# Hymba-style encoder block: one SBUF ring moved by 64 bytes, and four buffers of the up-projection swapped between two rings

## The chip, the cores and the metric

The kernel runs on one core of one Trainium2 chip. The metric is device time in microseconds (us) for one launch, that is for the whole block on one sequence of 2048 tokens. Less is better.

## The reference

```python
def mixer_layer(x, ...):          # convolution group and bidirectional gated linear attention (GLA)
    z = rms_norm(x, mix_norm) @ w_in
    ...
    return concat([y_conv, y_gla]) @ w_out

def memory_cross_attention(x, mem, ...):      # 4 heads of 256, 256 memory rows
    hq = rms_norm(x, xa_norm) @ w_xq
    km, vm = split(rms_norm(mem, mem_norm) @ w_xkv)
    p = softmax(einsum('bqhd,bmhd->bhqm', qh, kh) / 16)
    return einsum('bhqm,bmhd->bqhd', p, vh) @ w_xo

def sq_relu_mlp(x, ...):                      # 1024 -> 4096 -> 1024
    return square(relu(rms_norm(x, mlp_norm) @ w_up)) @ w_down

x = x + mixer_layer(x); x = x + memory_cross_attention(x); x = x + sq_relu_mlp(x)
out = rms_norm(x, final_norm)                 # x: (1, 2048, 1024), all float32
```

## The kernel before, in words

**Products.** Activations lie transposed, with features on the partitions. A product is kept near float32 accuracy by splitting each operand into a rounded part `hi` and a rest `lo` (`split`, line 112: ScalarE copies `hi`, VectorE subtracts to get `lo`) and adding three matmuls, hi·hi, hi·lo and lo·hi (`mm3`, lines 141 to 143; `product`, line 1009; the down-projection, line 1240). In `nc.tensor.matmul(ps, L, R)` the second argument is the stationary operand, 128 columns of weights that are loaded first, and the third is the moving operand, 256 or 512 columns. The profile writes a matmul as `out<-moving,stationary`, and drops digits from tile names: `a` is a tile of the ring A4, `g` of G4, `gt` of GT, `t` of T2, `st` of ST; `ps` and `pg` are PSUM tiles.

**Rings.** All working tiles come from one SBUF pool, `big`. Tiles with one tag share a ring of `bufs` equal buffers. Within a ring, buffers go to tiles in the order in which the program first writes them. The rings lie one after another in the order in which the program first uses them: T2 (7 buffers of 2048 bytes per partition), G4 (8 of 4096), GT (8 of 2048), RAW (3 of 4096), A4 (28 of 4096), SM (11 of 64), ST (2 of 8192), CV (3 of 4112) and GS (9 of 64). In the compiled program T2, G4, GT, RAW and A4 all start 64 bytes past a multiple of 128. SM is 704 bytes long, which is 64 past a multiple of 128, so ST starts on a multiple of 128. Every matmul operand lies at a multiple of 512 bytes from the start of its tile; its address mod 128 is therefore that of its ring.

**Stages, in order of the profile's time.** Up to 850 us: the keys' and values' weights folded with the memory (`kv_mm`; the moving operand `memT` is in GT, 256 wide), the input projection in two halves (in `vg`, the moving weights are 256 wide and lie in A4 and ST by turns), GLA and convolution. From 850 to 1060 us: `w_out` for four blocks of 512 tokens (`y_tiles` puts the moving operand of block 2 half into ST and half into GT). From 1060 to 1431 us: cross-attention in 8 steps of 256 tokens. `xa_scores` multiplies by the folded keys (512 wide, six of eight weight tiles in A4 and two in ST as the moving operand; the stationary operand is in A4, G4 or, for step 1, in GT). `xa_probs` transposes the probabilities and splits them into eight GT tiles `L["p"]`. `xa_out` and, for the last step, `xa_last` multiply them (moving, 256 wide, GT) by the folded values `wO` (stationary, A4 for six of eight tiles, G4 for two).

**Up-projection**, 1431 to 2081 us: for each half `hf` of the tokens and each `f` of 16 pairs of weight tiles, seven Strassen-like products of 12 matmuls, numbered 1, 4, 5, 6, 2, 7, 3 in the order of the code. `weight_side(f + 1)` is written at the head of iteration f: it loads two weight tiles into RAW and CV, forms the sums t1, t2, t4, t3 on VectorE and splits everything: `ha`, `hc`, `hb` into G4, and the operand of product 3, `hd`, into two tiles of ring T, which is GT by default. `c1`, `u2`, `c11` and `c22` (all T2) collect the four outputs, which pass through the squared relu and go to HBM. The last `weight_side(0)` of the first half is written after the outputs of f = 15. `weight_side(0, T2)`, called once before the loop, has its sums and `hd` in T2.

**Down-projection**, 2081 to 2630 us: weights are loaded into T2 (`raw`, line 1164; half of the loads into GT) and split into G4; then the remainder and the final norm.

**Order of the work.** Except in blocks marked as a manual schedule, a planner reorders instructions when the kernel is built: it takes each engine's instructions as they become ready by its own costs, the earlier-written first, and an instruction that is the first to write a tile waits for that tile's turn in its ring. The order is then fixed, and each engine runs its list in that order. The up-projection and the cross-attention are ordered by the planner on all engines.

Of the kernel before, what the change touches and what calls it, by code (L numbers as in the profile page):

```python
# [9 lines left out]
F32 = mybir.dt.float32  # L10
F32R = mybir.dt.float32r
# [6 lines left out]
P = 128  # L18
# [12 lines left out]
def block_kernel(ctx, tc, x, mem, wm, wv, wlg, wlog, wout, wxk, wxv, wxqT, wxo, wup, wdn,  # L31
# [3 lines left out]
    big = ctx.enter_context(tc.tile_pool(name="big", bufs=1))  # L35
# [8 lines left out]
    def G4(dt=F32, shape=(P, 1024)):  # L44
        return big.tile(list(shape), dt, tag="g", name="g4", bufs=NG)
# [10 lines left out]
    def T2(dt=F32, shape=(P, 512)):  # L56
        return big.tile(list(shape), dt, tag="t2", name="t2", bufs=7)

    def GT(dt=F32, shape=(P, 512)):
        return big.tile(list(shape), dt, tag="gt", name="gt", bufs=8)  # L60
# [7 lines left out]
    def PS(shape=(P, 512)):  # L68
        return psp.tile(list(shape), F32, tag="ps", name="ps", bufs=4)

    def PG(shape=(P, 512)):
        return psp.tile(list(shape), F32, tag="pg", name="pg", bufs=4)
# [39 lines left out]
    def split(src, hi, lo):  # L112
        mark["act"] = nc.scalar.copy(hi, src)  # L113
        nc.vector.tensor_tensor(out=lo, in0=src, in1=hi.bitcast(F32), op=ALU.subtract)  # L114
# [403 lines left out]
    def mem_part(q):  # L518
        mt = G4(F32, (P, 4, NMEM))
        nc.sync.dma_start(mt, mem[q * TB:(q + 1) * TB, :].rearrange("(k p) t -> p k t", p=P))  # L520
        for j in range(2):
            hi, lo = GT(F32R, (P, 2, NMEM)), GT(F32R, (P, 2, NMEM))
            for i in range(2):
                kt = 4 * q + 2 * j + i
                if q == 0:
                    nc.scalar.activation(hi[:, i], mt[:, 2 * j + i], AF.Copy, scale=g_mem[:, kt:kt + 1])
                else:
                    nc.vector.tensor_scalar_mul(hi[:, i], mt[:, 2 * j + i], g_mem[:, kt:kt + 1])
                nc.vector.scalar_tensor_tensor(out=lo[:, i], in0=mt[:, 2 * j + i], scalar=g_mem[:, kt:kt + 1],
                                               in1=hi[:, i].bitcast(F32), op0=ALU.mult, op1=ALU.subtract)  # L530
            memT.append((hi, lo))
        return mt
# [126 lines left out]
    def x2_rows(b, i):  # L659
        nc.scalar.copy(rows[:, i], to_rows(rcol[:, 4 * b:4 * b + 4], PS))  # L660
# [99 lines left out]

    with tc.manual_schedule(engines={EngineType.PE}):
        mts = [mem_part(0)]
        ws = [load_w(wxk[0])]
        mts.append(mem_part(1))
        ws.append(load_w(wxk[1]))
        nc.sync.dma_start(cst, consts)
# [156 lines left out]
    def add(out, a, b, op=ALU.add, eng=nc.vector):  # L923
        eng.tensor_tensor(out=out, in0=a, in1=b, op=op)  # L924
# [15 lines left out]
    def R2():  # L940
        return [RAW(), CV()[:, :D]]
# [18 lines left out]
    def token_side(hf):  # L960

        a11 = quarter(hf, 0, 0, S2())
        a22 = quarter(hf, 1, 1, R2())
        a21 = quarter(hf, 1, 0, S2())
        yield None
        yield 1, operand(a11)
        yield 4, operand(a22)
        s = a22  # L970
        both(s, a21, a22, ALU.add)
        yield 5, operand(s)
        both(s, s, a11, ALU.subtract)
        yield 6, operand(s)
        both(a21, a11, a21, ALU.subtract)
        a12 = quarter(hf, 0, 1, S2())
        yield 2, operand(a12)
        yield 7, operand(a21)
        both(a12, a12, s, ALU.subtract)
        yield 3, operand(a12)  # L980

    def weight_side(f, T=GT):

        raw = R2()
        for i in range(2):
            nc.sync.dma_start(raw[i], wup[f + 16 * i])
        w11, w21, w12, w22 = raw[0][:, :TB], raw[0][:, TB:], raw[1][:, :TB], raw[1][:, TB:]
        ha, hc, hb = ([G4(F32R), G4(F32R)] for _ in range(3))
        t1, t2, t4, t3 = T(), T(), T(), T()
        hd = T(F32R), T(F32R)  # L990
        half = lambda h, i: (h[0][:, i * TB:(i + 1) * TB], h[1][:, i * TB:(i + 1) * TB])
        split(raw[0], *ha)
        add(t1, w12, w11, ALU.subtract)
        add(t2, w22, t1, ALU.subtract)
        add(t4, t2, w21, ALU.subtract)
        add(t3, w22, w12, ALU.subtract)
        split(t4, *half(hc, 0))
        split(t3, *half(hc, 1))
        split(t1, *half(hb, 0))
        split(t2, *half(hb, 1))  # L1000
        split(w22, *hd)
        return {1: half(ha, 0), 2: half(ha, 1), 5: half(hb, 0), 6: half(hb, 1), 4: half(hc, 0), 7: half(hc, 1), 3: hd}

    def product(ps, W, X, first):

        for kt in range(4):
            ks = slice(kt * P, (kt + 1) * P)
            for w, x in ((0, 0), (0, 1), (1, 0)):
                nc.tensor.matmul(ps, W[w][:, ks], X[x][kt], start=first and kt + w + x == 0,  # L1009
                                 stop=kt == 3 and w == 1, skip_group_check=not first)  # L1010

    def sq_relu(t, src, f, b):
        nc.scalar.activation(t, src, AF.Relu)
        nc.scalar.activation(t, t, AF.Square)
        nc.sync.dma_start(zu[f * P:(f + 1) * P, b * TB:(b + 1) * TB], t)

    def sq_relu_v(t, f, b):
        nc.vector.scalar_tensor_tensor(out=t, in0=t, scalar=0.0, in1=t, op0=ALU.max, op1=ALU.mult)
        nc.sync.dma_start(zu[f * P:(f + 1) * P, b * TB:(b + 1) * TB], t)
# [8 lines left out]
    for s in range(NS):  # L1028
        if s + 1 < NS:
            xa_scores(s + 1, 0, 0)  # L1030
            if s > 0:
                xa_probs(s, 0)
            xa_scores(s + 1, 0, 1)
            if s > 0:
                xa_probs(s, 1)
                x2_rstd(s - 1)
            xa_scores(s + 1, 1, 0)
            xa_scores(s + 1, 1, 1)
            if s == 0:
                xa_probs(s, 0)  # L1040
                xa_probs(s, 1)
        else:
            xa_probs(s, 0)
            xa_probs(s, 1)
            x2_rstd(s - 1)
            sides = [token_side(0)]
            next(sides[0])
            X = dict([next(sides[0])])
            W = weight_side(0, T2)
            X.update([next(sides[0])])  # L1050
            xa_last(s)
            f_last = sumsq(live[s]["xs"])
            continue
# [12 lines left out]
    for hf in range(2):  # L1066
        b0, b1 = 2 * hf, 2 * hf + 1
        if hf == 1:
            X = {}
        for f in range(16):  # L1070
            def x(i):
                if i not in X:
                    k, X[k] = next(sides[hf])
                    assert k == i
                return X[i]
            if f + 1 < 16:
                nxt = weight_side(f + 1)
            if hf == 0 and f == 14:
                sides.append(token_side(1))
                next(sides[1])  # L1080
            px, py, pz, pw = PS(), PG(), PS(), PG()
            product(px, W[1], x(1), True)
            c1 = T2()
            nc.scalar.copy(c1, px)
            product(pw, W[4], x(4), True)
            product(pz, W[5], x(5), True)
            product(py, W[6], x(6), True)
            u2 = T2()
            add(u2, py, c1)
            product(px, W[2], x(2), False)  # L1090
            c11 = T2()
            sq_relu(c11, px, f, b0)
            product(py, W[7], x(7), False)
            add(c1, py, c1)
            c22 = T2()
            add(c22, pz, c1)
            sq_relu(c22, c22, f + 16, b1)
            add(c1, c1, pw, ALU.subtract)
            sq_relu_v(c1, f, b1)
            product(pz, W[3], x(3), False)  # L1100
            add(u2, pz, u2)
            sq_relu_v(u2, f + 16, b0)
            if hf == 0 and f == 12:
                for i in range(2):
                    x2_rows(2 + i, i)
            if hf == 0 and f == 15:
                nxt = weight_side(0)
            W = nxt
# [282 lines left out]
```

## Time and profile before

| | |
|---|---|
| three runs | 2743.51, 2741.66, 2735.44 us; median 2741.66 |
| profiled execution | 2743.17 us, span of the trace 2741.3 us |
| mean granted TensorE clock | 0.976 |
| PE (matmul) busy | 2611.3 us, 95% of the span, 13560 matmuls |
| PEld (weight load) busy | 2224.7 us, 81% |
| DVE (VectorE), ACT (ScalarE), POOL (GpSimd) busy | 1632.1, 933.6, 396.7 us |

PE's busy time counts a matmul from its start to its modelled end, and consecutive matmuls overlap: the pace is the time from one start to the next, which a window full of one kind of matmul gives as its length over their count. A window also counts a matmul that reaches into it from before, so one matmul's duration is added to the length.

### The profile page before, as it was taken

How to read it: one execution, taken by the hardware profiler on the slowest of the kernel's cores; microseconds unless marked ns; L12 is line 12 of the kernel's file. 1: busy time of each engine (PE TensorE's matmuls, PEld its weight loads, DVE VectorE, ACT ScalarE, POOL GpSimd, SP SyncE). 2: the span in 40 equal slices, each digit the busy share in tenths (PEclk: the TensorE clock that was granted, in tenths of full speed). 3: DMA queues.
4: the chain of work that ended last, by engine and by line, in shares of the span. 5: the costliest groups of instructions: out<-in, count | busy, mean ns of one | idle time of the engine just before them, and what ended most of it. 6: DMA issues, size and time to landing. Idle time of an engine off the chain costs nothing.

```text
span 2741.3 us, 34734 instructions
## 1 busy us (share of the span) xinstructions
PE 2611.3 (95%) x13560; PEld 2224.7 (81%) x13560; DVE 1632.1 (60%) x2430; ACT 933.6 (34%) x1432; POOL 396.7 (14%) x250
## 2 busy tenths in 40 slices
PE   7999989989889999999998999899999999999998
PEld 6898878877677787989886888688887788878877
DVE  6412363467757455343467557765655767788975
ACT  5411153423435443232234333433333222222322
POOL 1000010112210000000021000300002425243323
PEclk9999999999899999999999999999999999999999
DMA  7512355223444452101134332343338664545233
GB/s 246 180 61 68 100 175 167 77 89 116 129 122 157 150 184 85 62 31 47 47 119 151 104 119 96 112 139 115 113 117 301 203 200 143 178 160 183 94 104 112
DMA packets 198308, 353.26 MB, mean 129 GB/s; under 512 B 17344, under 2 KB 73792, under 8 KB 198144
## 3 DMA queue, kind: packets, MB, share of 16 engines
q1 hardware_dynamic: 198144, 351.05, 39.7%
q8 instruction: 106, 1.74, 0.3%
q14 instruction: 58, 0.48, 0.1%
HBM read 262.90 MB, written 88.08 MB: 128 GB/s over the span
## 4 chain that ended last, share of the span: by engine, by line
PE 76%; DVE 9%; DMA 5%; issue 4%; ACT 3%; POOL 2%; SPq 0%; POOLq 0%; DVEq 0%; ACTq 0%
PE ps L1009 12%; PE ps L141 9%; PE ps L142 9%; PE ps L143 9%; PE pg L1009 9%; PE pg L1240 8%; PE ps L1240 8%; PE pg L141 3%; PE pg L143 3%; PE pg L142 3%; DVE a L114 2%; DMA gt<-zv 1%; DVE g L114 1%; DMA raw<-zy 1%; DVE g L396 1%
## 5 line engine op out<-in xcount | busy, mean ns | idle before, releaser
L141 PE MATMUL ps<-a,a 128*128 128x512 f32 (+1 forms) x840 | 306.8, 365 | 6.8 <-DVE t L245 6.8
L142 PE MATMUL ps<-a,a 128*128 128x512 f32 (+1 forms) x840 | 306.2, 364 | 0.0
L143 PE MATMUL ps<-a,a 128*128 128x512 f32 (+1 forms) x840 | 306.1, 364 | 0.0
L1009 PE MATMUL pg<-a,g 128*128 128x512 f32 x1152 | 287.3, 395 | 13.1 <-DVE t L924 6.1
L1240 PE MATMUL pg<-a,g 128*128 128x512 f32 x1176 | 288.5, 392 | 10.4 <-DVE a L924 7.9
L1240 PE MATMUL ps<-a,g 128*128 128x512 f32 x1176 | 285.4, 389 | 1.7 <-DVE a L924 1.7
L1009 PE MATMUL ps<-a,g 128*128 128x512 f32 x1152 | 277.5, 389 | 0.2 <-ACT a L113 0.2
L1240 PEld LDWEIGHTS pg<-a,g 128*128 128x128 f32 x1176 | 222.6, 190 | 58.1 <-issue 8.9
L1009 PEld LDWEIGHTS pg<-a,g 128*128 128x128 f32 x1152 | 219.4, 191 | 61.5 <-DVE t L924 6.6
L1240 PEld LDWEIGHTS ps<-a,g 128*128 128x128 f32 x1176 | 220.7, 188 | 48.0 <-DVE a L924 2.1
L1009 PEld LDWEIGHTS ps<-a,g 128*128 128x128 f32 x1152 | 216.0, 188 | 45.4 <-ACT a L113 0.6
L113 ACT CAST a<-raw 128x1024 fp32r<-128x1024 f32 (+1 forms) x126 | 127.7, 1021 | 363.4 <-PE ps L1240 122.0
L114 DVE TENSOR_TENSOR a<-raw,a 128x1024 fp32r<-128x1024 f32 (+1 forms) x126 | 158.5, 1264 | 119.8 <-ACT a L113 118.0
L113 ACT CAST g<-gt 128x512 fp32r<-128x512 f32 x180 | 103.6, 618 | 342.9 <-PE pg L1009 203.8
L141 PEld LDWEIGHTS ps<-a,a 128*128 128x128 f32 x840 | 162.3, 193 | 32.4 <-DVE t L245 4.8
L143 PEld LDWEIGHTS ps<-a,a 128*128 128x128 f32 x840 | 162.7, 194 | 23.2
L142 PEld LDWEIGHTS ps<-a,a 128*128 128x128 f32 x840 | 162.5, 193 | 23.4 <-issue 0.2
L149 POOL TENSOR_TENSOR sm<-sm,nhalf 128x2 f32<-128x2 f32 (+1 forms) x26 | 23.0, 886 | 924.0 <-DVE sm L147 924.0
L114 DVE TENSOR_TENSOR g<-gt,g 128x512 fp32r<-128x512 f32 x180 | 142.5, 830 | 8.4 <-ACT g L113 8.3
L924 DVE TENSOR_TENSOR t<-pg,t 128x512 f32<-128x512 f32 x64 | 44.0, 688 | 172.6 <-PE pg L1009 170.7
L924 POOL TENSOR_TENSOR gt<-gt,t 128x512 f32<-128x512 f32 x42 | 65.7, 1581 | 459.7 <-DMA t<-in_wdn 390.1
L114 DVE TENSOR_TENSOR g<-raw,g 128x1024 fp32r<-128x1024 f32 (+3 forms) x90 | 103.3, 1158 | 33.0 <-ACT g L113 31.6
(327 smaller groups left out, 5380.8 us busy)
## 6 DMA issues: line engine op xcount, KB each, us to landing
zu<-t SPq DMA_DIRECT2D x128, 256.0 KB, 3.2
raw<-zu SPq DMA_DIRECT2D x64, 512.0 KB, 3.9
t<-in_wdn SPq DMA_DIRECT2D x84, 256.0 KB, 3.5
raw<-in_wm SPq DMA_DIRECT2D x32, 512.0 KB, 3.8
raw<-in_wup SPq DMA_DIRECT2D x32, 512.0 KB, 3.5
cv<-in_wup SPq DMA_DIRECT2D x32, 512.0 KB, 4.3
cv<-zu SPq DMA_DIRECT2D x32, 512.0 KB, 5.0
cv<-zu SPq DMA_DIRECT2D x40, 256.0 KB, 4.1
```

The lines of the kernel that those rows point to most:

```text
L113: mark["act"] = nc.scalar.copy(hi, src)
L114: nc.vector.tensor_tensor(out=lo, in0=src, in1=hi.bitcast(F32), op=ALU.subtract)
L141: nc.tensor.matmul(ps, lh, rh, start=first, stop=False)
L142: nc.tensor.matmul(ps, lh, rl, start=False, stop=False)
L143: mark["pe"] = nc.tensor.matmul(ps, ll, rh, start=False, stop=last)
L149: nc.gpsimd.tensor_tensor(out=r, in0=v, in1=nhalf[:, :n], op=ALU.pow)
L396: nc.vector.tensor_tensor_scan(out=Q[hf][:, sl], data0=reset, data1=K[hf][:, sl], initial=0.0, op0=ALU.mult, op1=ALU.add)
L924: eng.tensor_tensor(out=out, in0=a, in1=b, op=op)
L1009: nc.tensor.matmul(ps, W[w][:, ks], X[x][kt], start=first and kt + w + x == 0, stop=kt == 3 and w == 1, skip_group_check=not first)
L1240: nc.tensor.matmul(ps, l, r, start=not chained and k == 0 and l is wh and r is x[k][0], stop=k == n - 1 and l is wl, skip_group_check=chained)
```

## The change

Two new tiles of 64 bytes, `gap0` and `gap1`, are never written. The first is requested just before the first GT tile and the second just after the first pair, so that in the pool's order the GT ring has 64 bytes ahead of it and the rings after it have 128 more than before. GT would then start on a multiple of 128; T2, G4, RAW, A4 and ST would keep their addresses mod 128. Of the up-projection's tiles, `hd` goes from GT to T2, and the outputs `c11` and `c22` go from T2 to GT.

```diff
@@ def mem_part(q):
         for j in range(2):
+            if q == j == 0:
+                big.tile([P, 16], F32, tag="gap0", name="gap0", bufs=1)
             hi, lo = GT(F32R, (P, 2, NMEM)), GT(F32R, (P, 2, NMEM))
+            if q == j == 0:
+                big.tile([P, 16], F32, tag="gap1", name="gap1", bufs=1)
@@
-    def weight_side(f, T=GT):
+    def weight_side(f, T=GT, TD=T2):
@@
         t1, t2, t4, t3 = T(), T(), T(), T()
-        hd = T(F32R), T(F32R)
+        hd = TD(F32R), TD(F32R)
@@
-            c11 = T2()
+            c11 = GT()
             sq_relu(c11, px, f, b0)
@@
-            c22 = T2()
+            c22 = GT()
             add(c22, pz, c1)
```

No instruction is added or removed, and no matmul changes its size.

## The prediction

> **What bounds the kernel now.** I read the page's first and fourth parts first. PE is busy for nearly all of the span and carries three quarters of the chain that ended last, so a microsecond of matmul pace is a microsecond of time wherever PE runs without gaps.
>
> ```profile
> span 2741.3 us, 34734 instructions
> PE 2611.3 (95%) x13560; PEld 2224.7 (81%) x13560; DVE 1632.1 (60%) x2430; ACT 933.6 (34%) x1432; POOL 396.7 (14%) x250
> PE 76%; DVE 9%; DMA 5%; issue 4%; ACT 3%; POOL 2%; SPq 0%; POOLq 0%; DVEq 0%; ACTq 0%
> ```
>
> Next, busy times in three windows that are each full of one kind of 256-wide matmul: the input projection with its moving operand in ST, the same projection (same line, shapes and stationary blocks) with it in A4, and the cross-attention's output with the probabilities in GT.
>
> ```profile
> core 0: us, PE busy (x) PEld busy (x) DVE busy (x) ACT busy (x) POOL busy (x), PEclk, DMA share, GB/s
> 180.00:200.00 20.00, 20.00 (x179) 20.00 (x178) 3.99 (x8) 0.03 (x1) 0.00 (x0) 1.00 0.33 106
> 201.00:221.00 20.00, 20.00 (x169) 20.00 (x168) 2.83 (x8) 0.00 (x0) 0.00 (x0) 1.00 0.14 48
> 1095.00:1112.00 17.00, 17.00 (x144) 17.00 (x143) 3.24 (x7) 2.12 (x2) 0.00 (x0) 1.00 0.19 63
> ```
>
> PE and the weight load are both busy throughout, at full clock. With 0.28 us added for the matmul that reaches in, the pace is 20.28/179 = 113.3 ns in the first, 20.28/169 = 120.0 in the second, 17.28/144 = 120.0 in the third. A4 and the stationary blocks are both 64 past a multiple of 128 bytes; ST is on a multiple. So a 256-wide matmul is 6.7 ns quicker where the two operands lie 64 apart mod 128, and the probabilities are today in the slow arrangement. One miscounted instruction is 0.6 ns, so 6.7 +- 0.6.
>
> At 512 columns it is the other way round. The timeline has twelve matmuls with ST moving between these two starts, and twelve of the up-projection (A4 moving, G4 stationary, equal mod 128) between the next two:
>
> ```profile
> 950.32 0.39 PE L141 MATMUL ps<-st,a 128*128 128x512 f32 x1
> ...
> 953.12 0.39 PE L141 MATMUL ps<-gt,a 128*128 128x512 f32 x1
> ...
> 1563.58 2.88 PE L1009 MATMUL ps<-a,g 128*128 128x512 f32 x12
> 1566.30 2.88 PE L1009 MATMUL pg<-a,g 128*128 128x512 f32 x12
> ```
>
> 2.80/12 = 233.3 ns against 2.72/12 = 226.7: 64 apart costs 6.7 ns there.
>
> **The shift of GT, by its matmuls.** Groups by line and form give the counts (each product has three lines; I show one where they agree):
>
> ```profile
> L141 PE MATMUL pg<-gt,a 128*128 128x256 f32 x360 | 102.6, 285 | 0.4 <-DVE gt L114 0.4
> L141 PE MATMUL pg<-gt,g 128*128 128x256 f32 x120 | 34.0, 283 | 0.0
> L141 PE MATMUL ps<-gt,a 128*128 128x256 f32 x88 | 26.3, 305 | 10.8 <-ACT a L113 10.0 <-ACT gt L113 0.9
> L141 PE MATMUL ps<-gt,g 128*128 128x256 f32 x72 | 21.7, 302 | 3.0 <-ACT g L113 3.0
> L143 PE MATMUL ps<-gt,g 128*128 128x256 f32 x72 | 21.6, 300 | 3.6 <-DVE g L114 3.6
> L141 PE MATMUL ps<-gt,a 128*128 128x512 f32 x32 | 12.5, 390 | 0.0
> L141 PE MATMUL ps<-a,gt 128*128 128x512 f32 x24 | 9.4, 390 | 0.0
> L141 PE MATMUL ps<-st,gt 128*128 128x512 f32 x8 | 3.2, 394 | 0.0
> L1009 PE MATMUL ps<-a,gt 128*128 128x512 f32 x372 | 95.2, 406 | 4.5 <-DVE t L924 4.5
> L508 PE MATMUL pg<-cst,gt 128*128 128x128 f32 x64 | 11.6, 295 | 4.4 <-DVE gt L502 4.4
> ```
>
> *Probabilities.* 8 steps x 8 outputs x 8 memory tiles x 3 = 1536 matmuls: (360 + 120) x 3 into `pg`, and 96 of the `ps` rows, from the last step. They wait for almost nothing (0.4 us in 1440). Some 18 of the last step run at half clock and gain nothing. 1518 x 6.7 = **-10.2**; I take -10.0, from 1518 x 6.1 = -9.3 to 1518 x 7.3 = -11.1.
>
> *Memory operand.* The other (88 + 72) x 3 - 96 = 384 matmuls are `memT` against `wxk` and `wxv`. At most 384 x 6.7 = -2.6. But the rows show PE waiting 10.8, 3.0 and 3.6 us there for weights that ACT and DVE have just split after a load. Those arrive when they arrive, so PE would only wait longer. I take -0.2; ends -2.6 and 0.
>
> *`w_out`, block 2.* GT moving against A4, 512 wide, 3 x 32: 96 x 6.7 = **+0.6**. *Step 1's scores*, GT stationary: 72 with A4 moving lose, 24 with ST moving win: 48 x 6.7 = **+0.3**. *Product 3*: were `hd` to stay in GT, its 372 matmuls would cost +2.5; in T2, equal mod 128 to A4, it costs nothing. *Fp32 transposes of GLA* (64, line 508): no equal pair of rows at 128 columns; bounded by 64 x 6.7 = 0.4 either way, taken as 0. GLA's other GT products have both operands in GT.
>
> The shift sums to -10.0 - 0.2 + 0.6 + 0.3 = **-9.3**. It stays off nobody's path: the next waits in the cross-attention are DVE's, and DVE is 19% busy (3.24 of 17 us) in the third window.
>
> **The swap of rings.** Nothing is issued more or less often, but the planner gets other queues for buffers. After the change T2 hands out, per f, two `hd`, `c1`, `u2` (4 of 7 buffers), and GT the four sums, `c11`, `c22` (6 of 8). Four places matter.
>
> *Steady iterations.* Now:
>
> ```profile
> 1554.43 0.68 DVE L924 TENSOR_TENSOR gt<-gt,raw 128x512 f32<-128x512 f32 x1
> ...
> 1556.37 1.22 DVE L114 TENSOR_TENSOR g<-raw,g 128x1024 fp32r<-128x1024 f32 x1
> 1557.51 0.68 DVE L924 TENSOR_TENSOR t<-ps,t 128x512 f32<-128x512 f32 x1
> 1558.25 2.58 PEld L1009 LDWEIGHTS ps<-a,gt 128*128 128x128 f32 x12 [0.26 <-DVE t L924]
> 1558.26 3.00 PE L1009 MATMUL ps<-a,gt 128*128 128x512 f32 x12
> ...
> 1569.22 0.69 DVE L924 TENSOR_TENSOR t<-pg,t 128x512 f32<-128x512 f32 x1 [6.04 <-PE pg L1009]
> ```
>
> Product 3 starts after the addition into `c22`, which stands behind a 1.22 us split on DVE, and takes 3.00 - 2.88 = 0.12 us longer than its neighbours. After the change the sums of f + 2 come after `c22` of f in GT, so the sums that DVE does just before (the last two, 0.68 us each, from 1554.43) move behind, and `c22` can come first. 0 to 28 x 0.12 = -3.4; I take half, **-1.5**. `hd` no longer waits for the product 3 before it. `c1` of f + 1 now queues behind the second `hd` of f + 2, and so until product 3 of f ends, 1561.3; it is next needed by the addition after product 6, at 1569.22.
>
> *Start of the stage.* `hd` of f = 1 comes after the last sum of squares in T2, so its two splits (0.6 us on ACT, 0.7 on DVE) fall into the stretch in which PE waits for that sum:
>
> ```profile
> 1444.03 0.61 PE L157 MATMUL pg<-vec,t 128*128 128x1 f32 x4 [4.04 <-DVE t L651]
> ```
>
> 0 to +1.3; I take **+0.5**.
>
> *End of the stage.* Here PE waits for the first weights of the down-projection:
>
> ```profile
> 2061.64 5.16 SPq L1215 DMA_DIRECT2D a<-x2d  x7
> ...
> 2068.73 0.69 DVE L924 TENSOR_TENSOR t<-pg,t 128x512 f32<-128x512 f32 x1 [6.13 <-PE pg L1009]
> ...
> 2073.53 1.42 SPq L1168 DMA_DIRECT2D t<-in_wdn  x3
> ...
> 2080.44 1.93 ACT L113 CAST g<-t 128x512 fp32r<-128x512 f32 x3 [2.64 <-DMA t<-in_wdn]
> 2081.11 0.74 PE L1240 MATMUL pg<-a,g 128*128 128x512 f32 x2 [2.50 <-ACT g L113]
> ```
>
> The loads into T2 are written in the code before the `x2d` loads, yet go out 12 us later: they queue behind `c11` and `c22` in T2. After the change they queue only behind `u2` (2068.73), with three buffers free: 4.8 us earlier, more than the 2.50 us that PE waits. **-2.5**; ends -2.9 and 0 if another load is then late.
>
> *Between the halves.* Before, the sums of the second half's first tile are done at 1729.9, 30 us before product 4 needs them. After, they come behind `c22` of f = 15:
>
> ```profile
> 1729.22 0.69 DVE L924 TENSOR_TENSOR gt<-cv 128x512 f32<-128x512 f32 x1
> ...
> 1752.24 4.48 PE L1009 MATMUL pg<-a,g 128*128 128x512 f32 x12 [6.14 <-DVE t L924]
> ...
> 1759.29 0.84 PE L1009 MATMUL pg<-a,g 128*128 128x512 f32 x3
> ...
> 1762.36 0.68 DVE L924 TENSOR_TENSOR t<-ps,t 128x512 f32<-128x512 f32 x1
> ...
> 1763.09 5.49 PE L1009 MATMUL ps<-a,gt 128*128 128x512 f32 x12 [2.96 <-DVE t L924]
> ```
>
> `c22` is written at 1762.36. Three sums (2.0) and a split on ACT (0.6) later product 4 can start, at 1765.7; product 3, ready at 1763.1, covers 2.7 us of it. DVE does the moved 2.7 us later instead of earlier, which may shorten the 6.14 us wait. From -3 to +5; I take **+1.5**.
>
> Sum of the swap: -1.5 + 0.5 - 2.5 + 1.5 = -2.0. Together -9.3 - 2.0 = -11.3, against the profiled execution's own 2743.17 us (span and 1.9 around it): 2731.9. The median of the three runs shown is 1.5 lower, 2741.66: 2730.4. I predict **2731 us**.
>
> **Rivals.** *(A) The shift works, the planner's new order eats part of it.* For it: PE's waits around 1440 and 1752 hang on the order in DVE's queue. Against: steady iterations leave DVE idle for 6.04 us in one piece (1569.22). With +5 between the halves, +1.3 at the start and nothing won elsewhere: 2741.7 - 9.3 + 6.3 = 2739.
>
> *(B) The address has no effect, or the unwritten tiles get no space.* The ST rows could be faster for another reason (their DMA share is 0.33, not 0.14). Against: the third window paces like the second at a share of 0.19, and the sign turns at 512 columns. Time: 2741.7 - 2.0 = 2740. The Trainium skill speaks for this: "TensorE: Matmul & The Clock Gate", Part 2, says that "Loading the next tile's weights doesn't steal SBUF read bandwidth from the running matmul." By that rule the shift would be worth 0; the trace's 113.3 against 120.0 ns disagrees with it.
>
> *(C) Slower: the second half starts without its weights.* Products 4, 5, 6 and 7 need the late sums. If DVE's fixed list has the token side's splits ahead of them (eight, as long as the 1.22 us split above, or longer), PE waits 10 to 20 us, and PE's half clock after a long wait (3.00 us becomes 5.49 above) adds some 5: at +20, 2741.7 - 9.3 - 0.5 + 20 = 2752. It decides from 12 us of waiting on. Against: PE has products 1, 3 and 2, 8 us, to do meanwhile.
>
> **Chances and range.** Forecast 0.60, with its own range 2724 to 2736; (A) 0.20; (B) 0.08; (C) 0.12. Outcomes within 0.3% (8.2 us) of 2741.7 are what a measurement of this kernel hardly tells from no change; the three runs alone spread over 8.1 us. Faster than 2733.4: most of the forecast's case, 0.61. Within: 0.29, from (A), (B) and the forecast's upper edge. Slower than 2749.9: 0.10, from (C). The range, 2719 to 2745, takes the terms' favourable ends (-11.1 - 3.4 - 2.9 - 3 and the memory operand's -2.6) at the bottom and most of (A) and (B) at the top.
>
> **What would show it.** In the profile after: windows full of `pg<-gt,a` at 113 ns and not 120; `ps<-gt,a` 512 wide at 233; product 3 written `ps<-a,t` at 227; `t<-in_wdn` issued soon after the last `u2`, and no wait of 2.5 us at the first matmul of line 1240; between the halves a wait on sums or splits no longer than today's. The prediction is wrong if the pace of the probabilities stays at 120, or if PE waits over 10 us more between the halves.

## The result and the profile after

The changed kernel takes 2760.09 us (median of 4 runs, 2757.21 to 2761.41) against 2742.59 us for the kernel before on the same chip (4 runs, 2735.44 to 2744.08). The ratio is 1.0066, with a 95% interval of 1.0049 to 1.0083: 17.5 us slower, where 11 us faster was predicted. The profiled execution took 2760.86 us.

The page of the changed kernel, its first and fifth parts (line numbers are 4 higher than before):

```profile
span 2758.7 us, 34726 instructions
PE 2630.8 (95%) x13560; PEld 2219.3 (80%) x13560; DVE 1626.2 (59%) x2430; ACT 933.0 (34%) x1432; POOL 395.9 (14%) x250
...
L1244 PE MATMUL pg<-a,g 128*128 128x512 f32 x1176 | 293.9, 396 | 11.9 <-DVE a L928 10.6
L1013 PE MATMUL pg<-a,g 128*128 128x512 f32 x1152 | 291.5, 402 | 10.0 <-DVE t L928 7.9
```

The same two groups on the page of the kernel before:

```profile
L1240 PE MATMUL pg<-a,g 128*128 128x512 f32 x1176 | 288.5, 392 | 10.4 <-DVE a L924 7.9
L1009 PE MATMUL pg<-a,g 128*128 128x512 f32 x1152 | 287.3, 395 | 13.1 <-DVE t L924 6.1
```

The same 13560 matmuls keep PE busy for 2630.8 us, 19.5 us longer than the 2611.3 us before, and the span grows by 17.4 us. Its idle time is 127.9 us, against 130.0. So PE does not wait more: matmuls have become slower. The next view, a window full of the probabilities' matmuls, shows that it is not these:

```profile
core 0: us, PE busy (x) PEld busy (x) DVE busy (x) ACT busy (x) POOL busy (x), PEclk, DMA share, GB/s
1092.00:1108.00 16.00, 16.00 (x144) 16.00 (x143) 2.94 (x7) 2.12 (x2) 0.00 (x0) 1.00 0.21 67
```

(16.00 + 0.28)/144 = 113.1 ns, as predicted, where it was 120.0 at the same full clock. The loss is in the up- and the down-projection. The up-projection's timeline after the change:

```profile
1559.90 2.95 PE L1013 MATMUL pg<-a,g 128*128 128x512 f32 x12
1562.70 2.95 PE L1013 MATMUL ps<-a,g 128*128 128x512 f32 x12
1565.49 2.94 PE L1013 MATMUL pg<-a,g 128*128 128x512 f32 x12
...
1570.13 2.96 PE L1013 MATMUL ps<-a,t 128*128 128x512 f32 x12
1572.93 1.09 PE L1013 MATMUL ps<-a,g 128*128 128x512 f32 x4
```

From 1562.70 to 1565.49 twelve matmuls take 2.79 us, 232.5 ns each; before, twelve took 2.72 us, 226.7 each. Product 3, now with its stationary operand in T2, takes 2.80/12 = 233.3. No row names a wait, and nothing about these instructions changed except where A4 lies and, for product 3, which ring holds the stationary operand.

**What is different about A4.** In the compiled programs T2 and G4 start at 8384 and 22720 in both kernels. A4 starts at 84160 before and at 84288 after: the two unwritten tiles of 64 bytes push everything behind GT by 128 bytes. Mod 128 that is nothing; mod 256 A4 now lies 128 off G4 and T2. The table gives the mean time from the start of one matmul to the start of the next, worked out by matching every matmul of a trace with the addresses of its two operands in the compiled program (steps with a stall, above 300 ns at 512 columns or 200 at 256, left out). The distance is the moving operand's address less the stationary operand's, mod 256:

```
moving, stationary (columns)        count   before: distance, ns   after: distance, ns
A4, G4 up-projection (512)           2304        0    226.8           128    232.7
A4, GT then T2, product 3 (512)   372/384        0    227.6           128    232.4
A4, G4 down-projection (512)         2352        0    226.7           128    232.4
A4, G4 other stages (512)             720        0    228.1           128    232.5
G4, A4 w_out (512)                    384        0    227.1           128    232.3
A4, A4 (512)                         1800        0    227.5             0    227.4
ST, G4 scores (512)                   144      192    233.7            64    230.3
GT, A4 (256)                         1344        0    120.1           192    114.7
GT, G4 (256)                          576        0    120.0            64    115.6
ST, A4 (256)                          384      192    113.4           192    113.4
```

The rows whose distance did not change kept their pace (A4 with A4, ST with A4). The first five rows, 6144 matmuls, lost 2304 x 5.9 + 384 x 4.8 + 2352 x 5.7 + 720 x 4.4 + 384 x 5.2 ns = 13.6 + 1.8 + 13.4 + 3.2 + 2.0 = 34 us. The probabilities won some 8 us.

Now the four places of the swap. At the end of the up-projection, the timeline after:

```profile
2068.76 2.24 SPq L1172 DMA_DIRECT2D t<-in_wdn  x3
...
2073.02 0.69 DVE L928 TENSOR_TENSOR t<-pg,t 128x512 f32<-128x512 f32 x1 [6.34 <-PE pg L1013]
...
2078.33 2.28 PE L1244 MATMUL pg<-a,g 128*128 128x512 f32 x9
...
2081.47 0.50 PE L1244 MATMUL pg<-a,g 128*128 128x512 f32 x1 [0.86 <-ACT g L113]
...
2081.81 2.95 PE L1013 MATMUL ps<-a,t 128*128 128x512 f32 x12
...
2147.47 4.46 PE L1244 MATMUL pg<-a,g 128*128 128x512 f32 x12 [8.62 <-DVE a L928]
```

The loads `t<-in_wdn` do go out earlier, ahead of the last `u2`, and the 2.50 us that PE waited for the first weights shrink to 0.86. The planner has also put ten matmuls of the down-projection ahead of the up-projection's last product 3 (2081.81), which before came ahead of all of them. But 66 us later PE waits 8.62 us for an addition of DVE. In the kernel before, PE waits 5.22 us at the same matmul:

```profile
2141.06 4.58 PE L1240 MATMUL pg<-a,g 128*128 128x512 f32 x12 [5.22 <-DVE a L924]
```

The experiments below show how these hang together.

### The profile page after: what moved, and what is told of

Read it like the earlier page. It is cut to its first block, busy times and chain, and to the rows that moved or that the text cites. A ratio compares the mean times of both kernels' runs of the same rounds, so it can differ in the third digit from the quotient of the medians.

```text
span 2758.7 us, 34726 instructions
## 1 busy us (share of the span) xinstructions
PE 2630.8 (95%) x13560; PEld 2219.3 (80%) x13560; DVE 1626.2 (59%) x2430; ACT 933.0 (34%) x1432; POOL 395.9 (14%) x250
## 4 chain that ended last, share of the span: by engine, by line
PE 57%; DVE 7%; DMA 5%; issue 3%; POOL 2%; ACT 2%; SPq 0%; POOLq 0%; DVEq 0%; ACTq 0%
PE ps L1013 12%; PE pg L1013 9%; PE pg L1244 8%; PE ps L1244 8%; PE ps L141 4%; PE ps L143 4%; PE ps L142 4%; PE pg L143 2%; PE pg L141 2%; PE pg L142 2%; DVE a L114 2%; DMA gt<-zv 1%; DVE g L114 1%; DMA t<-in_wdn 1%; POOL st L928 1%
## 5 line engine op out<-in xcount | busy, mean ns | idle before, releaser
L1244 PE MATMUL pg<-a,g 128*128 128x512 f32 x1176 | 293.9, 396 | 11.9 <-DVE a L928 10.6
L1013 PE MATMUL pg<-a,g 128*128 128x512 f32 x1152 | 291.5, 402 | 10.0 <-DVE t L928 7.9
L1244 PE MATMUL ps<-a,g 128*128 128x512 f32 x1176 | 291.6, 395 | 1.4 <-DVE a L928 1.4
L1013 PE MATMUL ps<-a,g 128*128 128x512 f32 x1152 | 289.2, 395 | 3.4 <-ACT g L113 2.1
```

The lines of the kernel that those rows point to most:

```text
L1244: nc.tensor.matmul(ps, l, r, start=not chained and k == 0 and l is wh and r is x[k][0], stop=k == n - 1 and l is wl, skip_group_check=chained)
```

## The experiments

Two theories stood against each other. **D256**: the pace of a matmul follows the distance between its moving and its stationary operand mod 256; the gaps put A4 at a bad distance. **ORDER**: the planner's new order, from the swap of rings, costs the time. In the labels, two numbers are the bytes of the first and the second gap.

**The swap alone.**

```diff
-                big.tile([P, 16], F32, tag="gap0", name="gap0", bufs=1)
+                pass
...
-                big.tile([P, 16], F32, tag="gap1", name="gap1", bufs=1)
+                pass
```

> The two 64-byte tiles are left out; hd in T2 and c11, c22 in GT as in the change. Theory D256 (the pace of a matmul follows the difference of its operands' addresses mod 256, and the change set A4 128 bytes off G4, T2 and GT's neighbours by pushing everything behind GT by 128): the up- and down-projection pace at 227 ns again, and the swap alone gives the -2 of the prediction or a little more: 2735 to 2742. Theory ORDER (the planner's new order after the swap is what costs): the loss stays, 2742.6 + 17.5 + 9 = 2769, with PE waits of over 20 us more in the up-projection.

2744.12 us (2742.00 to 2747.70, 11 runs) against 2740.52; ratio 1.0013, interval 1.0003 to 1.0022. The swap costs about 3.6 us, against an expectation of a small gain. That is about a fifth of the loss.

**The gaps alone**, with the rings of `hd`, `c11` and `c22` as before:

```diff
-        hd = TD(F32R), TD(F32R)
+        hd = T(F32R), T(F32R)
-            c11 = GT()
+            c11 = T2()
-            c22 = GT()
+            c22 = T2()
```

> The two 64-byte tiles of the change, rings of the up-projection as before. D256: the pace of A4 against G4 is 232 ns as in the changed kernel (about 6000 matmuls x 5.4 = +33 us), the probabilities pace at 113 to 114 ns (-9); what is missing against the changed kernel is what the swap gives: 2760 to 2768. ORDER: only the gain of the shift is left, 2742.6 - 9.3 = 2733.

2755.94 us (2750.94 to 2761.61, 6 runs); ratio 1.0056, interval 1.0040 to 1.0072. The unwritten tiles, which move no data and add no instruction, carry 15.4 us of the loss. Nor do they change the order: in its trace PE, DVE, ACT and POOL run the same instructions in the same order as in the kernel before. That excludes ORDER as the main cause.

**The changed kernel with other gaps**: 64 and 192 bytes, or 192 and 64. Both bring A4 back to a distance of 0 mod 256 from G4 and T2. GT is then 64 past A4 in the one and 192 past it in the other.

```diff
-                big.tile([P, 16], F32, tag="gap1", name="gap1", bufs=1)
+                big.tile([P, 48], F32, tag="gap1", name="gap1", bufs=1)
```

> As the change, with the second tile of 192 bytes, so that everything behind GT moves by 256 and A4 lies as far from G4 and T2 mod 256 as before; GT lies +64 from both. D256: up- and down-projection at 227 ns, the probabilities between 113 and 117 ns: 2760 - 33 = 2727, at most 2732. ORDER: as the change, 2760. If the modulus is 512 and not 256, A4 against G4 is still off: 227 would not come back.

2738.11 us (2735.42 to 2746.39, 11 runs); ratio 0.9992, interval 0.9981 to 1.0003.

```diff
-                big.tile([P, 16], F32, tag="gap0", name="gap0", bufs=1)
+                big.tile([P, 48], F32, tag="gap0", name="gap0", bufs=1)
```

> As the change, with the first tile of 192 bytes: again everything behind GT moves by 256, but GT lies 192 (that is -64) from G4 and A4, the difference that ST has to A4 in the kernel before. D256: 227 ns for A4 against G4 and 113.4 ns for all probabilities, 2 ns better than +64 if the sign matters (1536 x 2 = 3 us): 2724 to 2730. ORDER: 2760.

2736.36 us (2730.79 to 2739.54, 11 runs); ratio 0.9980, interval 0.9970 to 0.9989. Against the changed kernel 128 bytes more in one gap win 23.7 us (2760.09 - 2736.36), or 21.7 with each taken against the runs of the kernel before that were made beside it (17.5 lost, 4.2 won). In the two timelines the loss lies where D256 puts it: of 24.5 us between the two spans, 13.6 are in the up-projection (from its first matmul to the first of the down-projection), 7.8 in the down-projection, 2.5 ahead of both. The 256-wide matmuls tell the two signs apart. Windows of 12 us full of the probabilities' matmuls with the kernels in this order, 64 then 192:

```profile
1092.00:1104.00 12.00, 12.00 (x104) 12.00 (x103) 2.39 (x5) 2.12 (x2) 0.00 (x0) 1.00 0.27 89
```

```profile
1092.00:1104.00 12.00, 12.00 (x109) 12.00 (x108) 2.64 (x6) 1.06 (x1) 0.00 (x0) 1.00 0.27 88
```

12.28/104 = 118.1 ns against 12.28/109 = 112.7 ns (by all matched steps 117.8 and 114.2). So GT 192 past A4, which is 64 short of it, is the better place. Mod 128 the two are the same.

**No swap, gaps of 192 and 64**: the change without its second half, with the distance set right.

> No swap; 192 bytes ahead of GT and 64 behind it, so that GT alone is off (-64 mod 256 from G4, A4 and T2). D256: probabilities -10, product 3 pays because hd stays in GT (384 x 3 to 6.6 ns = +1.2 to +2.5), w_out and scores +1: 2740.5 - 7 = 2733 to 2735, and the down-projection's first wait as in the kernel before (5 us, not 9). If the swap was worth having, this is slower than the same gaps with it (2736).

2734.91 us (2730.98 to 2738.70, 6 runs) against 2742.72; ratio 0.9974, interval 0.9961 to 0.9987. It beats both kernels, by 7.8 us the one before. From the same gaps with the swap (0.9980) it can't be told apart, since the intervals overlap. Its timeline:

```profile
1565.67 3.06 PE L1013 MATMUL ps<-a,gt 128*128 128x512 f32 x12
1568.57 2.68 PE L1013 MATMUL pg<-a,g 128*128 128x512 f32 x11
1571.08 2.88 PE L1013 MATMUL ps<-a,g 128*128 128x512 f32 x12
1573.80 2.88 PE L1013 MATMUL pg<-a,g 128*128 128x512 f32 x12
```

The products with A4 and G4 are back at 2.72/12 = 226.7 ns.

**No swap, one gap of 128 bytes ahead of GT.** GT and A4 keep their distance to each other, and both lie 128 off G4.

```diff
             if q == j == 0:
+                big.tile([P, 32], F32, tag="gap0", name="gap0", bufs=1)
             hi, lo = GT(F32R, (P, 2, NMEM)), GT(F32R, (P, 2, NMEM))
```

> No swap; one gap of 128 bytes ahead of GT and none behind, so that GT and A4 both move by 128 and keep their distance to each other, while both are 128 from G4 and T2. GT's addresses mod 128 are as before. D256: 512-wide A4 against G4 at 232 ns, about 5700 x 5.4 = +31; the probabilities at 120 against A4: 2740.5 + 31 = 2771, and 2766 to 2775. If only the address mod 128 counts: 2740.5, unchanged.

2757.57 us (2756.43 to 2760.15, 4 runs); ratio 1.0055, interval 1.0039 to 1.0070. The expectation, 2766 to 2775, had the place right and the size wrong. The matmuls lose 5760 x 5.6 = 32 us (the 6144 less product 3, which stays at distance 0), but they are not all on the path: between matmuls of the same count in the two traces the up-projection is 11.0 us longer and the down-projection 10.1. The time grows by 14.9 us; in this trace the stages ahead of the cross-attention also ended 5.3 us earlier, which no edit here accounts for.

**No swap, odd distances.** Gaps of 32 and 224, then of 96 and 160 bytes: A4 stays at 0, GT goes to 32 and 96 past it.

> No swap; 32 bytes ahead of GT, 224 behind. D256: A4 against G4 at 227 ns. GT is 32 off both: the probabilities' pace between 113 and 120 ns, product 3 between 227 and 234. A dependence on whether two addresses fall in the same 64-byte piece would show 120, one on the same 32-byte piece 113 to 117.

> No swap; GT 96 bytes off G4 and A4. D256: A4 against G4 at 227 ns; the probabilities between the 115.6 ns of +64 and the 118.6 ns of 128, product 3 between 230 and 234.

One run each: 2737.78 us and 2747.61 us, beside 2742.72 for the kernel before. The probabilities take 117.0 ns at a distance of 32 and 120.1 at 96. For 96 a pace between those at 64 and 128 had been expected; it is above both (117.8 and 119.6). The pace falls from 120.0 at 0 to 117 or 118 at 32 and 64, and is back near 120 at 96 and 128. Product 3 takes 233.1 at a distance of 224 and 234.3 at 160.

**All rings 128 bytes further on.** D256 speaks of distances; but in every slow kernel so far A4 itself started at 84288. This kernel puts A4 there, and keeps all distances of before.

```diff
-    one = T2()[:, :P]
+    big.tile([P, 32], F32, tag="gap0", name="gap0", bufs=1); one = T2()[:, :P]
```

> The kernel before with one unwritten tile of 128 bytes ahead of the first T2 tile, so that all rings lie 128 bytes further on: A4 then starts at 84288, exactly as in the changed kernel and in ring_128_0, and every distance between two rings is the one of before. Distance theory (the pace follows the distance between moving and stationary operand mod 256): 12 matmuls of the up-projection in 2.72 us, probabilities at 120 ns, the time within 0.3% of before. Rival, place theory (the pace follows the place of A4 itself mod 256, which is where after and ring_128_0 lost): 2.79 us for 12 matmuls and about 2757 us.

2742.72 us (2740.46 to 2744.22, 10 runs) against 2742.06; ratio 1.0002, interval 0.9993 to 1.0011. Its timeline:

```profile
1721.73 2.88 PE L1009 MATMUL ps<-a,g 128*128 128x512 f32 x12
1724.45 2.88 PE L1009 MATMUL pg<-a,g 128*128 128x512 f32 x12
1727.17 2.88 PE L1009 MATMUL ps<-a,g 128*128 128x512 f32 x12
```

2.72 us for twelve, with A4 at the same address as in the slow kernels. The place alone does nothing; the distance does it.

**The swap, half by half.** `swap_only` showed a loss of 3.6 us where a gain of 2.0 was predicted. First its own traces. The timeline of the swap alone, the queue of SP, PE, DVE and POOL:

```profile
1553.30 2.89 PE L1013 MATMUL ps<-a,t 128*128 128x512 f32 x12
1556.03 1.07 PE L1013 MATMUL ps<-a,g 128*128 128x512 f32 x4
...
2059.61 2.02 SPq L1172 DMA_DIRECT2D t<-in_wdn  x3
...
2068.80 2.44 PE L1244 MATMUL pg<-a,g 128*128 128x512 f32 x9
...
2072.37 0.50 PE L1244 MATMUL pg<-a,g 128*128 128x512 f32 x1 [1.12 <-ACT g L113]
...
2072.71 2.90 PE L1013 MATMUL ps<-a,t 128*128 128x512 f32 x12
...
2108.64 7.42 DVE L114 TENSOR_TENSOR g<-gt,g 128x512 fp32r<-128x512 f32 x3
2113.77 7.90 POOL L928 TENSOR_TENSOR gt<-t,gt 128x512 f32<-128x512 f32 x4
...
2120.44 0.68 DVE L928 TENSOR_TENSOR a<-pg,a 128x512 f32<-128x512 f32 x1
...
2124.07 3.40 DVE L928 TENSOR_TENSOR raw<-raw,st 128x1024 f32<-128x1024 f32 x1 [1.75 <-POOL st L928]
...
2134.10 1.28 DVE L114 TENSOR_TENSOR g<-t,g 128x512 fp32r<-128x512 f32 x2
...
2138.99 5.46 PE L1244 MATMUL pg<-a,g 128*128 128x512 f32 x12 [8.80 <-DVE a L928]
```

The down-projection's first matmul starts 12.3 us earlier on the clock (2068.8 against 2081.1), but ten of its matmuls now run ahead of the up-projection's last product 3 (2072.71). Counted over the same matmuls, all of the up-projection and the first twelve of the down-projection, PE is 8.1 us earlier, of which the last stretch of the up-projection has won 3.0. But the down-projection's first group of products is not bound by PE. There DVE splits the weights and adds into the accumulators while POOL forms the sums of the next weights, and the two hold each other up: a split of 128x512 takes 7.42/3 = 2.47 us with POOL at work, and 1.28/2 = 0.64 us when POOL has stopped. So although PE comes to this stage 8.1 us earlier, the addition that it needs is done only some 2 us earlier than before (2138.99 against 2141.06), and PE waits 8.80 us instead of 5.22. The Trainium skill says this in "SBUF — State Buffer", section "Who interferes with whom": "A DVE instruction with two SBUF inputs contends with a GpSimd instruction that reads SBUF". The trace agrees, with 2.47 against 0.64 us; an addition that has one of its inputs in PSUM (2120.44) takes 0.68 us in the midst of POOL's work.

Is it the outputs' move that does both? One kernel has only `hd` in T2, the other only `c11` and `c22` in GT, both without gaps.

> No gaps; only hd goes to T2, while c11 and c22 stay in T2. Theory END (what the swap wins at the head of the down-projection comes from c11 and c22 leaving T2, and so does what it then loses): the loads into T2 still queue behind c11 and c22, PE waits about 2.5 us for the first weights and about 5.2 us at the second row of groups as before; 2738 to 2743. Rival HD (the order of T2's buffers changes with hd, and the loss comes from that): a wait of 8 to 9 us near 2140 and about 2744.

> No gaps; only c11 and c22 go to GT, while hd stays in GT too. Theory END: the first weights of the down-projection come 4 to 8 us earlier, and the next wait on DVE near 2140 grows from 5.2 to 8 or 9 us, so that little or nothing is left: 2741 to 2746, much as swap_only. Rival HD: the wait near 2140 stays at 5 us and the earlier start is kept: 2735 to 2738. Apart from that GT then has all eight of its buffers asked for by each f (four sums, two hd, c11, c22), and if that holds up weight_side the waits of the up-projection grow: above 2746.

`c11` and `c22` alone: 2742.36 us (2737.96 to 2746.81, 12 runs), ratio 1.0002, interval 0.9992 to 1.0012. PE in its timeline:

```profile
2073.02 0.49 PE L1240 MATMUL pg<-a,g 128*128 128x512 f32 x1 [0.23 <-DVE g L114]
...
2138.98 4.95 PE L1240 MATMUL pg<-a,g 128*128 128x512 f32 x12 [8.81 <-DVE a L924]
```

The wait for the first weights is gone and the later one is 8.81: theory END, with the gain paid back. `hd` alone: 2750.22 us (2745.77 to 2757.77, 10 runs), ratio 1.0034, interval 1.0023 to 1.0046, which neither theory expected. Its longest wait for DVE at the head of the down-projection is 5.8 us, not the 8 or 9 of rival HD. Its timeline at the start of the up-projection:

```profile
1458.06 2.56 PE L1009 MATMUL pg<-a,g 128*128 128x512 f32 x10 [1.65 <-DVE a L114]
...
1467.28 0.69 DVE L924 TENSOR_TENSOR t<-ps,t 128x512 f32<-128x512 f32 x1 [2.86 <-DMA zu<-t]
1468.03 4.51 PE L1009 MATMUL ps<-a,t 128*128 128x512 f32 x12 [2.87 <-DVE t L924]
```

With `hd`, `c1`, `u2`, `c11` and `c22` all in T2, DVE has to wait 2.86 us until an output has left for HBM before it may write the next buffer, and PE waits 2.87 us for DVE. This is the loss that moving `c11` and `c22` away avoids in the full swap.

Stages of the traces, as the difference in length to the kernel before (us; a stage runs from one matmul to another of the same count):

```
stage                                          length  after  swap   c only  hd only  192/64+swap  192/64
cross-attention (matmuls 5540 to 7700)          333.2   -6.5   0.0   -0.0     0.0      -7.6        -7.6
up-projection, f = 0 and 1                       50.3   +1.0  -0.5   -0.3    +4.4      +0.9        +0.9
up-projection, f = 2 to 13                      231.7   +4.6  -1.1   -1.1    +0.5      -1.1        +0.5
up-projection, from mid f = 15 to f = 17         66.7   +1.8  +0.9   +3.8    +2.0      +1.5        -0.0
up-projection, f = 18 to 30                     249.0   +5.1  -1.3   -1.2    +1.3      -1.2        +0.6
f = 31 and down-projection, matmuls 0 to 12      26.4   -2.9  -3.0   -3.6    +0.5      -3.1        +1.8
down-projection, matmuls 12 to 100               19.9   +0.5  -0.0   +0.0    +0.7      +0.0        +0.0
down-projection, matmuls 100 to 1176            253.0   +9.7  +7.1   +5.8    +0.7      +6.9        +0.1
down-projection, the rest                       270.6   +4.9  +1.4   +0.1    -0.1      +0.3        +1.1
```

Where `c11` and `c22` are in GT, ten or twelve matmuls of the down-projection stand ahead of the up-projection's last product; so the row of f = 31 runs on to the twelfth, by when all kernels have done the same work. In these four columns the 2.9 to 3.6 us won there are followed by 5.8 to 9.7 us lost between matmuls 100 and 1176. Of the 9.7 of the changed kernel some 5 are the slower pace (the kernel with one gap of 128 and no swap loses 4.9 in this row). The part up to matmul 5540 is left out: it ends between 1051.3 and 1060.7 us in these traces, in no order of the edits.

## Why the prediction was wrong

The step that failed stands in the prediction and in what it started from: addresses were reduced **mod 128**, and so "equal mod 128" was taken for "same place". The paces that were compared could not show this to be wrong, since all those pairs lie at 0 or at 192 mod 256, and those are 0 and 64 mod 128. The trace of before has one pair that could: A4 moving against ST (48 matmuls between 574 and 597 us) lies at 64, and its mean step is 229.9 ns, where ST moving against A4, at 192, takes 233.8. Mod 128 both are 64 apart. The term "everything behind GT moves by 128 bytes" was never priced, because by that rule it was 0. It measured +34 us of PE time and some 22 to 24 us of the time. Neither of the two signs that the prediction named for being wrong appeared: the probabilities' pace went to 113.1 ns, and no wait between the halves grew by 10 us. It had watched GT's matmuls and PE's waits, and the loss came in matmuls of A4 that nobody meant to move. The shift of GT by itself, with A4 kept at 0 and without the swap, won 7.8 us where -9.3 was forecast; product 3 with `hd` still in GT is paid for in that.

The points one by one:

- *Probabilities, -10.0.* They came, smaller: -7.6 us over the cross-attention where A4 stays at 0 against G4. The pace taken over from ST (113.3) holds in the best window (113.1), but the mean over all steps is 114.2 with A4 and 115.1 with G4 (gaps of 192 and 64): 1440 x 5.7 = -8.2. In the changed kernel G4 is at 64 to GT instead of 192, and the scores with A4 and G4 at 128: -6.5.
- *Memory operand, -0.2* (ends -2.6 and 0). Not settled, as the stages ahead of the cross-attention end up to 9 us apart from one trace to the next. The 10.8 us of waits for split weights are unchanged (first row).

```profile
L141 PE MATMUL ps<-gt,a 128*128 128x256 f32 x88 | 26.3, 305 | 10.8 <-ACT a L113 10.0 <-ACT gt L113 0.9
L141 PE MATMUL ps<-gt,a 128*128 128x512 f32 x32 | 12.6, 394 | 0.0
```

- *`w_out`, block 2, +0.6*, and *step 1's scores, +0.3*: right. GT moving at 512 columns is the second row above, 394 ns each where it was 390; its pace went from 228.5 to 233.2 ns, 96 x 4.7 = +0.5, and A4 moving against GT from 227.8 to 230.3, 72 x 2.5 = +0.2.
- *Product 3 in T2 "costs nothing"*: wrong, and by the failed step itself: T2 is at 128 to the moved A4, and 384 x 4.8 = +1.8 us.
- *Steady iterations, -1.5*: right in mechanism and under-sized. The swap alone wins 1.1 + 1.3 us in f = 2 to 13 and 18 to 30, and so does moving `c11` and `c22` alone, so it is `c22` that comes earlier. With `hd` alone nothing is won. Product 3 went from 3.00 us to 2.89 in both. In the changed kernel the slower pace covers it (+4.6 and +5.1).
- *Start of the stage, +0.5*: -0.5 with the swap. `hd` alone costs 4.4, which the prediction had not seen, but the swap does not pay it.
- *End of the stage, -2.5*: there, and near the size that was forecast (-3.0 with the swap alone, -2.9 in the changed kernel), but given back. The prediction allowed for the case that "another load is then late"; what was late was DVE beside POOL in the first group of the down-projection, at +7.1 us with the swap alone, more than the gain. Why it is more than the gain, and not just as much, these runs don't show.
- *Between the halves, +1.5*: +0.9 with the swap, +1.8 in the changed kernel, inside the range. Its waits after the change are those that were foreseen, a wait for a sum and one for a split:

```profile
1749.01 5.49 PE L1013 MATMUL pg<-a,g 128*128 128x512 f32 x12 [5.68 <-DVE t L928]
1760.41 4.58 PE L1013 MATMUL ps<-a,t 128*128 128x512 f32 x12 [2.99 <-DVE gt L928]
1767.54 0.50 PE L1013 MATMUL ps<-a,g 128*128 128x512 f32 x1 [2.06 <-ACT g L113]
```

Of the rivals, (A), the planner eating part of the gain, is what the kernel with gaps of 192 and 64 did, at 2736 us where the rival said 2739; but it was eaten in the down-projection, not between the halves. (B) fell, since the address has an effect and the unwritten tiles get their space. The rule of the Trainium skill that spoke for it ("TensorE: Matmul & The Clock Gate", Part 2) would let no such difference be expected. Measured was one: the pace goes from 112.7 to 120 ns at 256 columns and from 226.8 to 232.7 at 512 by where the two operands lie to each other. What makes it so isn't shown. (C) ended on the right side for another reason: its wait of 12 us or more between the halves is not in the trace.

Of the 34 us of slower matmuls about 10 are hidden. In the up-projection nearly all is paid (13.6 us of 2304 x 5.9 + 384 x 4.8 ns = 15.4), ahead of it 2.5 of 5.2. In the down-projection 7.8 of 13.4 is paid; about 2 of the other 5.6 went into shorter waits of PE there (13.3 us in the changed kernel, 15.3 with gaps of 192 and 64). Where the rest went wasn't separated.

## What to carry to other kernels

Before an address is changed, list every pair of moving and stationary operand with its distance and its count, and price all of them: a gap moves every ring behind it, and here the pairs nobody meant to move were four times as many as those that were meant. A modulus read from two residues is a guess until a third residue has been seen; a shift by a full period of the guessed modulus, with nothing else changed, is the cheap test. And a stage that starts earlier only helps if the engine that binds its first part, here DVE beside POOL, gets its work earlier too.

## What the runs showed of the hardware

The pace of a stream of matmuls, each with its own weight load, depends on the distance between the moving and the stationary operand's addresses mod 256, and differently for the two widths. These are the lowest and the highest mean step of any pair, over all kernels shown (256 columns: moving in GT, ST or A4; 512: all pairs of rings but those named below):

```
distance mod 256   256 columns, ns   512 columns, ns
  0                119.8 - 120.4     226.7 - 229.4
 32                116.9 - 117.1     233.1
 64                115.5 - 117.9     229.2 - 230.8
 96                120.1 - 120.2     233.7 - 234.9
128                118.6 - 119.6     232.3 - 233.0
160                not run           233.4 - 234.3
192                113.4 - 115.1     233.0 - 233.8
224                not run           232.9 - 233.1
```

At 512 columns an equal address is best: the blocks in G4 take 226.8 ns at 0, with A4 moving in the up-projection, 230.3 at 64, with ST moving, and 232.7, or 2.6% more, at 128. At 256 columns the best place measured is 192, the moving operand 64 bytes short of the stationary one, by 6 ns or 5% against 0. It isn't symmetric: 64 past it gives 117.8 where 64 short gives 114.2. (The 115.5 at 64 is that of the blocks in G4 with gaps of 64 and 64, which stand between blocks in A4 at 192.) The shift of all rings by 128 bytes left every pace as it was.

Two short blocks are left out at 0, since the steps scatter after a change of pair. Product 3 of the kernel with one gap of 128 stands between products at a distance of 128: its mean is 230.4 ns, the medians of its first seven steps go up to 245, and only those of the next four are 227. ST moving against GT in step 1's scores, six matmuls at a time, has a mean of 231.7 to 231.9 at 0 and doesn't settle. So the table holds for long streams.

What in the memory or the engine makes it so, no run here shows. The period could also be a multiple of 256. One finding speaks against 512: with gaps of 192 and 64 bytes A4 lies 256 bytes further from G4 than before, and the pace in both projections is 226.8 to 226.9 ns, as before. Other multiples can't be told apart by these runs.
